# A list schedule that starts earlier in each layer of a two-layer encoder: v and g section, stores, and the order of attention and MLP steps

## The chip, the cores and the metric

The kernel runs on one core of a Trainium2 chip. The metric is device time in microseconds (us) of one execution: the median of 3 runs before the change is 1656.25 us, from 1655.57 to 1656.78 us.

## What is computed

Two layers (`DEPTH = 2`) on 512 tokens of width 1024, everything in float32. Each layer is a token part and a channel part. The reference, cut to that:

```python
for i in range(DEPTH):
    proj = x @ w_in[i]
    q_na, k_na, v_na, q_r, k_r, v_r, g_r, gate_a, gate_b = jnp.split(proj, IN_SPLITS, axis=-1)
    ya = neighbourhood_attention(q_na, k_na, v_na, na_rpb[i])          # 8 heads
    yb = bidirectional_retention(q_r, k_r, v_r, g_r, decay_f, decay_b)  # 4 heads
    merged = sigmoid(gate_a) * (ya @ w_branch_a[i]) + sigmoid(gate_b) * (yb @ w_branch_b[i])
    x = layer_norm(ALPHA * x + merged @ w_out[i], ln1_g[i], ln1_b[i])
    ffn = conv_glu_ffn(x, w_up[i], conv_w[i], conv_b[i], w_down[i])
    ple = sigmoid(x @ w_ple_gate[i]) * (p[i] @ w_ple_proj[i])
    x = layer_norm(ALPHA * x + ffn + ple, ln2_g[i], ln2_b[i])
```

## The kernel before

**Products.** Every float32 factor is split into a high and a low part: ScalarE casts the tile to `hi`, VectorE subtracts to get `lo` (`split`, L740), and each product is three matmuls (`mm3`: hi by hi, hi by lo, lo by hi). The large products are cut further, in the manner of Strassen and Winograd, into blocks of seven half-size products with the step names a, c, t1, t2, d, t3 and t4. The operands of the steps t1, t2, t3 and d are sums of halves; those of the weights are made by transfers that add in flight (GpSimd's queue, POOL), the others by VectorE. Steps of a block share PSUM banks: t4, for example, goes on adding in the bank that t3 left, so it starts only when VectorE has read that bank.

**Weights** come in chunks of 128x1024 values (512 KB) over two DMA queues: SyncE's (SP, plain loads) and POOL's (the transfers that add). They land in `raw`, `rawa` or `rawt` tiles, then come the cast `hi` on ScalarE and the subtraction `lo` on VectorE, then the matmuls.

**The order of a layer.** First the v and g section: `vg` (L1369) runs the keys of `VG[l]` (L51, L52). A key such as `0t3` is step t3 of block 0; `ga2` is one block of the a gate; `p0` and `p1` (layer 0) are the two halves of the input embedding. Then the steps of `FILL[l]` (L46): `2a` to `8t4` are blocks 2 to 8 (gates, q and k), `R0` to `R3` one step of a retention head, `N0` to `N7` one step of an attention head. `ret_head` (L1497) has four steps for each head: scores `s` and the scaled transposed keys `kz`, the states `st` and `su`, the output `o`, and the transposed output `ybt`. After the output projection and the layer norm (`proj_ln`, L1136) comes the first MLP segment in `pg` (L2140), in the order of `PG[l]` (L58): the steps a to t4 without a number are the embedding's gate, `0a` to `1t4` two blocks of the up-projection, `g` one of four plain products of it, `S` and `T` the making of sums. Then `down` (L2109) and the later segments alternate. `sums_of` (L2007) makes the sums `ss` and splits them into `sh` and `sl`, which `down` reads; `R` are the four tiles in which the residual and all products of the channel part are added.

**Who orders what.** The program is recorded first (`Program`, L226). Where `prog.plan` is 0, each engine runs its instructions as they were written. Where it is `l + 1`, a planner orders them: `_dues` (L394) gives each instruction a due time, TensorE's own being the written order at the planner's costs, and `_order` (L484) builds a list schedule from the dues, with the buffers that are free (`CAP`, L71), how far ahead of its due a load may start (`load=16` and `load=17` in `SET`, L79) and, in layer 1, a random shake of the dues (`seed=2744, shake=0.4`). TensorE may draw a later step forward, up to `prog.win` products ahead. Before the change the planner takes over behind `vg`: `prog.plan, prog.win = l + 1, FILL_WIN` (L1847), and hands back in the last MLP segment (`prog.plan = 0`, L2234). All that touches an engine passes through the recorder, so L263 stands for nearly every instruction of the profile.

Of the kernel before, what the change touches and what calls it, by code (L numbers as in the profile page):

```python
# [17 lines left out]
T = 512  # L18
# [24 lines left out]

FILL_WIN = 10
FILL_AT = (36, 40, 56, 24, 28, 8, 20)
FILL = (tuple('2a 2c 7a 7c 2t1 7t1 7t2 2t2 7d 2d 2t3 7t3 2t4 7t4 3a 8a R0 8c R1 3c R0 3t1 8t1 R1 R0 R1 8t2 8d 8t3 R0 3t2 3d 8t4 3t3 4a R1 4c 3t4 5a R2 4t1 R2 5c R3 R3 5t1 4t2 R2 4d 5t2 R2 R3 5d R3 5t3 4t3 6a 6c 6t1 N0 N1 6t2 5t4 vn 6d N3 N1 6t3 4t4 6t4 N0 vn vn bb0 N2 vn bb2 N0 N2 N5 N1 N2 N3 N4 N6 bb3 bb1 N5 N6 N6 N4 bb4 N7 bb5 N4 N5 bb6 bb7 N3 xn N7 N7'.split()),  # L46
        tuple('2a 2c 7a 7c 2t1 7t1 7t2 2t2 7d 2d 2t3 7t3 2t4 7t4 3a 8a R0 8c R1 3c R0 3t1 8t1 R1 R0 R1 8t2 8d 8t3 R0 3t2 3d 8t4 3t3 4a R1 4c 3t4 5a R2 4t1 R2 5c R3 R3 5t1 4t2 R2 4d 5t2 R2 R3 5d R3 5t3 4t3 6a 6c 6t1 N0 N1 6t2 5t4 vn 6d N3 N1 6t3 4t4 6t4 N0 vn vn bb0 N2 vn bb2 N0 N2 N5 N1 N2 N3 N4 N6 bb3 bb1 N5 N6 N6 N4 bb4 N7 bb5 N4 N5 bb6 bb7 N3 xn N7 N7'.split()))
# [7 lines left out]

TABLES_AT = ('0t4', '1t4')

PG = (tuple('a 0a T S S c 0c S t1 g g S 1a t2 1c 0t1 0t2 1t1 1t2 0d 0t3 1d 1t3 d 0t4 1t4 g t3 t4 g'.split()),  # L58
        tuple('a 0a T S S c 0c S t1 g g S 1a t2 1c 0t1 0t2 1t1 1t2 0d 0t3 1d 1t3 d 0t4 1t4 g t3 t4 g'.split()))
# [19 lines left out]
SET = {1: dict(soon=5, hold=6, reserve=10, load=16, work=25, scale=1.0, spare=2, near=10, seed=0, shake=0.0), 2: dict(soon=5, hold=6, reserve=10, load=17, work=25, scale=1.0, spare=2, near=10, seed=2744, shake=0.4)}  # L79
ROUNDS = 12  # L80


# [3 lines left out]
def _up_order(l, s):  # L86

    return UP_ORDER[l][s - 1] if s else PG[l]

# [14 lines left out]
class Root:  # L104


    def __init__(self, pool, shape, dtype, kw, options):
        self.pool, self.shape, self.dtype, self.kw = pool, list(shape), dtype, kw
        self.buf = Buf(options, [self])
        self.tile, self.log = None, []  # L110

    def alloc(self):
        if self.tile is None:
# [180 lines left out]
class Flex(Root):  # L294


    def __init__(self, choices, shape, dtype, name):
        self.shape, self.dtype, self.choices, self.tile, self.log = list(shape), dtype, choices, None, []
        self.pool, self.kw, self.label = choices[0][0], None, name

    def choose(self, i):
# [51 lines left out]
def _jobs(ops):  # L353

    jobs, cur = [], None
    bufs = set()
    for seq, o in enumerate(ops):
        if o.eng is None:
            continue
        _costs(o)  # L360
        key = (o.plan, o.win, id(o.outs[0].root)) if o.eng == "tensor" else None
        after = set()
        for x, w in [(x, False) for x in o.ins] + [(x, True) for x in o.outs]:
            for y, w2, j in x.root.log:
                if (w or w2) and x.meets(y):
                    after.add(j)
        mine = {x.root.buf for x in o.ins}
        if key is not None and cur is not None and cur[0] == key and not any(a.seq > cur[1].seq for a in after) and (o.group and o.group == cur[2] or mine <= cur[1].bufs):
            j = cur[1]
            j.members.append(o)  # L370
            j.dur += o.dur
            j.after |= after - {j}
        else:
            j = o
            j.seq = seq
            j.after = after
            j.members = [o] if key is not None else None
            j.bufs = set()
            jobs.append(j)
            if o.eng == "tensor":  # L380
                cur = (key, j, o.group)
        for x, w in [(x, False) for x in o.ins] + [(x, True) for x in o.outs]:
            x.root.log.append((x, w, j))
            j.bufs.add(x.root.buf)
    seen = set()
    for j in jobs:
        j.takes = [b for b in j.bufs if b not in seen]
        seen |= j.bufs
        for b in j.bufs:
            b.left += 1  # L390
    return jobs


def _dues(jobs):  # L394

    soon = lambda j: SET[j.plan]["soon"] if j.plan else 5
# [290 lines left out]
def trunk(tc, wpack, x_nat, x_tr, head, p_tr, rpb, decay, ln_par, ln_col, conv, cos_t, sin_t, dist, xi_d, zd, mask, ident_d, out):  # L687
    prog = Program(tc)
# [4 lines left out]
    with ExitStack() as es:  # L693
# [109 lines left out]
        def fill_items(l):  # L803
# [389 lines left out]
        for i in range(2):  # L1193
            c = slice(i * 512, (i + 1) * 512)
# [118 lines left out]
        for l in range(DEPTH):  # L1313
# [55 lines left out]
            def vg(steps):  # L1369
# [22 lines left out]

                ws.deep = VG_DEEP
                for key in VG[l]:
                    for g in steps.get(key, ()):
                        r = next(g, None)
                        if isinstance(r, dict):
                            Sx.update(r)
# [13 lines left out]
                    elif kind == "c":  # L1412
                        w = two("w")
# [158 lines left out]
            qn, kn, kl, vn = {}, {}, {}, {}  # L1572
# [126 lines left out]
            xn = []  # L1699
# [266 lines left out]
            N1, N2 = slice(0, 512), slice(512, 1024)  # L1966
# [271 lines left out]
            for s in (len(SEGS) - 1,):  # L2238
# [142 lines left out]
                w, x4 = wx["w"], wx["x"]  # L2381
# [47 lines left out]
                t4 = products("t4", x4, s == 0)  # L2429
# [158 lines left out]
```

## Time and profile before

| | before |
|---|---|
| time, median of 3 runs | 1656.25 us |
| the profiled execution's own time | 1656.36 us |
| span of its instructions, first to last | 1654.6 us |
| TensorE (PE) matmuls | 1639.7 us busy, 9765 matmuls |
| VectorE (DVE) | 1309.3 us busy |
| ScalarE (ACT) | 999.1 us busy |
| GpSimd (POOL) | 280.4 us busy |
| transfers | 352.84 MB, mean 213 GB/s |

Stages of layer 0 by the trace: v and g section up to about 122 us, `FILL` up to about 370 us, output projection to 450 us, first MLP segment to 555 us, the rest to 850 us; layer 1 repeats that, and its v and g section ends at about 943 us.

How to read it: a row of a timeline gives start, length, engine, line, operation, output<-inputs, shapes and a count; in brackets stands the idle time of the engine ahead of it and who ended that. "Busy" of PE counts a matmul from its start to its modelled end, and the next one starts before that end, so PE can be late by some tenths of a us and still look busy.

### The profile page before, as it was taken

The numbers are of one execution on the slowest core, as the hardware profiler recorded it, in microseconds if no ns is written. First come the engines' busy times: TensorE is split into PE (matmuls) and PEld (weight loads), VectorE is DVE, ScalarE is ACT, GpSimd is POOL, SyncE is SP. The second block draws the span as 40 slices with busy tenths as digits, with TensorE's granted clock in tenths as the row PEclk, the third lists the DMA queues.
The fourth block names the chain that finished last, engine by engine and source line by source line (L and its number), as shares of the span: only waits on it lengthen the run. The fifth ranks groups of instructions, "written<-read, shape, count | busy, mean of one in ns | idle before, by whom it ended". The sixth has DMA issues, their size and how long they took to land.

```text
span 1654.6 us, 25522 instructions
## 1 busy us (share of the span) xinstructions
PE 1639.7 (99%) x9765; PEld 1460.0 (88%) x9765; DVE 1309.3 (79%) x1963; ACT 999.1 (60%) x1492; POOL 280.4 (17%) x328
## 2 busy tenths in 40 slices
PE   9999999999999999999999999999999999999997
PEld 7889999888889798898888899998888897988986
DVE  7757999687878968867876489997799789687688
ACT  6756667853557556455476566688445575663554
POOL 1111222210211111111112112221002111121113
PEclk9999999999999999999999999999999999999999
DMA  8997768865698898888688857787767987989884
GB/s 307 248 263 172 168 150 211 206 185 188 167 304 230 203 277 210 229 253 204 183 225 224 228 148 177 179 203 183 214 211 186 292 235 207 269 187 276 229 173 128
DMA packets 104827, 352.84 MB, mean 213 GB/s; under 512 B 11904, under 2 KB 16512, under 8 KB 104704
## 3 DMA queue, kind: packets, MB, share of 16 engines
q0 software_dynamic: 41040, 147.34, 46.1%
q1 hardware_dynamic: 63664, 203.86, 33.6%
q8 instruction: 77, 1.26, 0.3%
q14 instruction: 46, 0.38, 0.1%
HBM read 323.89 MB, written 25.69 MB: 211 GB/s over the span
## 4 chain that ended last, share of the span: by engine, by line
PE 91%; DVE 5%; DMA 2%; issue 1%; ACT 1%; POOL 0%; DVEq 0%; POOLq 0%; ACTq 0%
PE u L263 29%; PE gt L263 22%; PE v L263 15%; PE gn L263 8%; PE w L263 8%; PE o L263 2%; PE x L263 1%; DMA rawt<-in_wpack 1%; DVE lo L263 1%; PE ns L263 1%; PE na L263 1%; PE pt L263 1%; PE s L263 1%; PE tr L263 1%; PE st L263 1%
## 5 line engine op out<-in xcount | busy, mean ns | idle before, releaser
L263 DVE TENSOR_TENSOR lo<-rawa,hi 128x1024 fp32r<-128x1024 f32 (+1 forms) x198 | 235.9, 1199 | 69.7 <-ACT hi L263 69.6
L263 POOL DMA_DIRECT2D rawa<-in_wpack x150 | 133.7, 911 | 905.6 <-DVE lo L263 689.9
L263 ACT CAST hi<-rawa 128x1024 fp32r<-128x1024 f32 (+1 forms) x198 | 202.4, 1031 | 110.3 <-DMA rawa<-in_wpack 76.6
L263 DVE TENSOR_TENSOR lo<-raw,hi 128x1024 fp32r<-128x1024 f32 (+1 forms) x159 | 191.3, 1207 | 55.3 <-ACT hi L263 55.1
L263 PE MATMUL gt<-x1t,hi 128*128 128x512 f32 x640 | 197.5, 390 | 0.0
L263 ACT CAST hi<-raw 128x1024 fp32r<-128x1024 f32 (+1 forms) x159 | 163.9, 1038 | 48.7 <-PE gn L263 17.4
L263 PEld LDWEIGHTS gt<-x1t,hi 128*128 128x128 f32 x640 | 118.9, 188 | 23.7
L263 PE MATMUL gt<-x1t,lo 128*128 128x512 f32 x320 | 124.5, 389 | 0.0
L263 PE MATMUL u<-xt,hi 128*128 128x256 f32 x448 | 81.8, 284 | 0.0
L263 PE MATMUL u<-sh,hi 128*128 128x256 f32 x288 | 81.7, 284 | 0.0
L263 PE MATMUL v<-sh,hi 128*128 128x256 f32 x288 | 81.7, 284 | 0.0
L263 PE MATMUL v<-sh,lo 128*128 128x256 f32 x288 | 81.5, 283 | 0.0
L263 PE MATMUL v<-sl,hi 128*128 128x256 f32 x288 | 81.5, 283 | 0.0
L263 PE MATMUL u<-sl,hi 128*128 128x256 f32 x288 | 81.5, 283 | 0.0
L263 PE MATMUL u<-sh,lo 128*128 128x256 f32 x288 | 81.5, 283 | 0.0
L263 PE MATMUL gn<-hi,mt 128*128 128x512 f32 x256 | 80.2, 391 | 0.0
L263 ACT ACTIVATE uh<-u 128x512 f32<-128x512 f32 x60 | 35.8, 596 | 73.2 <-PE u L263 72.9
L263 PE MATMUL gt<-ybt,hi 128*128 128x512 f32 x256 | 79.6, 392 | 0.0
L263 ACT ACT_TABLE_LOAD x46 | 59.0, 1283 | 24.6 <-DVE sl L263 9.6
L263 PE MATMUL v<-hi,sl 128*128 128x512 f32 x184 | 72.0, 391 | 1.1 <-DVE sl L263 1.1
L263 PE MATMUL v<-hi,sh 128*128 128x512 f32 x184 | 71.8, 390 | 0.3 <-ACT sh L263 0.3
L263 PE MATMUL v<-lo,sh 128*128 128x512 f32 x184 | 71.7, 390 | 0.0
(302 smaller groups left out, 4873.6 us busy)
## 6 DMA issues: line engine op xcount, KB each, us to landing
raw<-in_wpack SPq DMA_DIRECT2D x155, 512.0 KB, 6.2
rawa<-in_wpack POOLq DMA_DIRECT2D x144, 512.0 KB, 7.1
rawa<-in_wpack SPq DMA_DIRECT2D x48, 512.0 KB, 6.8
rawt<-in_wpack SPq DMA_DIRECT2D x48, 512.0 KB, 5.4
rawt<-in_wpack POOLq DMA_DIRECT2D x48, 512.0 KB, 8.9
hi<-in_wpack POOLq DMA_DIRECT2D x40, 512.0 KB, 6.4
lo<-in_wpack POOLq DMA_DIRECT2D x40, 512.0 KB, 6.2
sx<-s_scr SPq DMA_DIRECT2D x32, 512.0 KB, 8.8
```

The lines of the kernel that those rows point to most:

```text
L263: r = o.call(*[real(x) for x in o.a], **{k: real(v) for k, v in o.k.items()})
```

## The change

The planner takes over earlier: in layer 0 at the key `ga2` of the v and g section, in layer 1 at its first key `0a`. Up to the end of `vg`, TensorE keeps the written order there (`prog.win = 1`); VectorE, ScalarE and the two DMA queues are ordered by due time. In `_dues`, nothing is due later than the last product of its plan, and a store to DRAM is due 5 us behind the instruction that makes its data, where it was due by its reader before. `FILL` and `PG` have new orders in both layers, and the shake of layer 1 and its `load=17` go. The other hunks only assert, while recording, that what is read was written. The instructions of the arithmetic and the transfers stay the same, in number and size; ScalarE has 49 table loads (`ACT_TABLE_LOAD`) where it had 46.

```diff
@@ FILL (the entry of layer 1) @@
-        tuple('2a 2c 7a 7c 2t1 7t1 7t2 2t2 7d 2d 2t3 7t3 2t4 7t4 3a 8a R0 8c R1 3c R0 3t1 8t1 R1 R0 R1 8t2 8d 8t3 R0 ...
+        tuple('7a 2a 2c 7c 2t1 7t1 7t2 7d 2t2 2d 2t3 7t3 2t4 7t4 3a 8a R0 R0 3c 8c 3t1 R1 8t1 R1 R0 R1 8t2 R0 8d 8t3 ...
@@ PG (the entry of layer 1) @@
-        tuple('a 0a T S S c 0c S t1 g g S 1a t2 1c 0t1 0t2 1t1 1t2 0d 0t3 1d 1t3 d 0t4 1t4 g t3 t4 g'.split()))
+        tuple('a 0a T S c S 0c 1a g g S 1c t1 0t1 S 0t2 t2 0d 0t3 1t1 0t4 1t2 1d 1t3 d 1t4 g t3 g t4'.split()))
@@ new @@
+VG_PLAN = ("ga2", "0a")
@@ SET @@
-... 2: dict(soon=5, hold=6, reserve=10, load=17, work=25, scale=1.0, spare=2, near=10, seed=2744, shake=0.4)}
+... 2: dict(soon=5, hold=6, reserve=10, load=16, work=25, scale=1.0, spare=2, near=10, seed=0, shake=0.0)}
@@ _dues @@
-    _dues.end = now
+    ends = {j.plan: j.due for j in jobs if j.eng == "tensor"}
+    for j in jobs:
+        if j.plan:
+            j.due = min(j.due, ends[j.plan])
+            if j.dma and j.after and not any(x.parts is not None for x in j.outs):
+                j.due = min(j.due, max(a.due + a.dur for a in j.after) + soon(j))
@@ vg @@
                 for key in VG[l]:
+                    if key == VG_PLAN[l]:
+                        _Ordered.on = set()
+                        prog.plan, prog.win = l + 1, 1
@@ trunk, behind vg @@
-            _Ordered.on = set()
-            prog.plan, prog.win = l + 1, FILL_WIN
+            prog.win = FILL_WIN
```

**Place 1: VectorE at the end of the v and g section of layer 0.** The rows `p` are the additions that free the banks `u` behind step `1t3` for step `1t4`; `lo` are subtractions for later weights. Before:

```order
L263 TENSOR_TENSOR lo_944<-rawa_209,hi_943 128x1024
L263 TENSOR_TENSOR u_158_921<-u_158_921,v_765 128x512
L263 TENSOR_TENSOR u_159_922<-u_159_922,v_766 128x512
L263 TENSOR_TENSOR lo_967<-rawa_211,hi_966 128x1024
L263 TENSOR_TENSOR lo_985<-rawa_929,hi_984 128x1024
L263 TENSOR_TENSOR p_141_804<-p_141_804,u_341 128x512
L263 TENSOR_TENSOR p_141_804<-p_141_804,u_342 128x512
```

The same place now:

```order
L264 TENSOR_TENSOR u_148_921<-u_148_921,v_768 128x512
L264 TENSOR_TENSOR lo_968<-rawt_162_693,hi_955 128x1024
L264 TENSOR_TENSOR u_149_932<-u_149_932,v_778 128x512
L264 TENSOR_TENSOR lo_998<-rawa_209,hi_986 128x1024
L264 TENSOR_TENSOR p_132_806<-p_132_806,u_341 128x512
L264 TENSOR_TENSOR p_132_806<-p_132_806,u_342 128x512
L264 TENSOR_TENSOR lo_1016<-rawa_211,hi_1007 128x1024
L264 TENSOR_TENSOR lo_1032<-rawa_786,hi_1030 128x1024
```

Between the additions `u` and the additions `p` stood two subtractions `lo`; behind the last `u` there is one now, and the others follow `p`.

**Place 2: VectorE at the start of the first `down` of layer 1.** Three pairs of sums are split there; `sl` is the low half of a pair, `ss` the sums of the third pair, `R<-R,u` the first results of `down` and `R<-R,psg` gated embeddings. Before:

```order
L263 TENSOR_TENSOR lo_14121<-rawa_13727,hi_14109 128x512
L263 TENSOR_TENSOR sl_14127<-ss_14034,sh_14116 128x1024
L263 SCALAR_TENSOR_TENSOR ss_14107<-ss_14107,gg_13355 128x256
L263 TENSOR_TENSOR ss_14107<-gg_13355 128x256
L263 SCALAR_TENSOR_TENSOR ss_14107<-ss_14107,gg_13355 128x256
L263 TENSOR_TENSOR R_13112<-R_13112,u_14047 128x512
L263 TENSOR_TENSOR R_13116<-R_13116,u_14060 128x512
L263 TENSOR_TENSOR sl_14153<-ss_14107,sh_14145 128x1024
```

The same place now:

```order
L264 TENSOR_TENSOR sl_14104<-ss_14039,sh_14069 128x1024
L264 SCALAR_TENSOR_TENSOR ss_14095<-ss_14095,gg_13343 128x256
L264 TENSOR_TENSOR ss_14095<-gg_13343 128x256
L264 SCALAR_TENSOR_TENSOR ss_14095<-ss_14095,gg_13343 128x256
L264 TENSOR_TENSOR sl_14124<-ss_14043,sh_14106 128x1024
L264 TENSOR_TENSOR R_13109<-R_13109,u_14048 128x512
L264 TENSOR_TENSOR sl_14141<-ss_14095,sh_14129 128x1024
L264 TENSOR_TENSOR R_13127<-R_13127,u_14062 128x512
L264 TENSOR_TENSOR lo_14158<-rawa_13659,hi_14121 128x1024
L264 TENSOR_TENSOR R_13895<-R_13895,psg_14037 128x512
L264 TENSOR_TENSOR R_13891<-R_13891,psg_14057 128x512
```

The sums `ss` of the third pair now precede the second `sl`, and one addition to `R` moved behind the third; two multiplications of `R` by `psg` come after all three. On TensorE, `PG` now ends in `g t4` where it ended in `t4 g`: 24 matmuls of step t4 stand between the last plain product, from which the third pair is made, and `down`.

**Place 3: ScalarE in the retention heads of layer 1.** The rows `kz` scale the keys of head 1, from which TensorE makes the states `st`; `qx` is an operand of head 0's output `o`, and `wx` are decays. Before:

```order
L263 ACTIVATE kz_9957<-kz_9866,zeta 128x128 x4
L263 ACT_TABLE_LOAD
L263 ACTIVATE p_1520_9781<-p_1520_9781 128x512
L263 CAST a_9998<-ta_9845 128x512
L263 CAST a_10001<-ta_9854 128x512
L263 COPY p_1555_10007<-v_9931 128x512
L263 CAST su_10009<-st_9912 128x512
L263 CAST qx_10018<-t_1497_9674 128x512
```

The same place now:

```order
L264 ACTIVATE kz_9976<-kz_9926,zeta 128x128 x4
L264 ACT_TABLE_LOAD
L264 ACTIVATE wx_9978<-xi_sb,lgs 128x256
L264 CAST qx_10011<-t_1497_9658 128x512
L264 ACTIVATE wx_9978<-wx_9978 128x384
L264 ACTIVATE wx_9978<-xi_sb,lgs 128x256
L264 CAST hi_10030<-raw_9964 128x1024
L264 CAST a_10044<-ta_10025 128x512
L264 CAST qx_10055<-t_1510_9739 128x512
L264 CAST su_10073<-st_9998 128x512
```

The decays of head 1 moved behind its `kz`. On TensorE, 84 matmuls stood between the transposes of these keys and the states `st`; now 36 do, 24 of step `8t1` and 12 of the scores.

More of the change, by code (lines that the diff above doesn't have):

```diff
@@ L45 @@
 FILL_AT = (36, 40, 56, 24, 28, 8, 20)
-FILL = (tuple('2a 2c 7a 7c 2t1 7t1 7t2 2t2 7d 2d 2t3 7t3 2t4 7t4 3a 8a R0 8c R1 3c R0 3t1 8t1 R1 R0 R1 8t2 8d 8t3 R0 3t2 3d 8t4 3t3 4a R1 4c 3t4 5a R2 4t1 R2 5c R3 R3 5t1 4t2 R2 4d 5t2 R2 R3 5d R3 5t3 4t3 6a 6c 6t1 N0 N1 6t2 5t4 vn 6d N3 N1 6t3 4t4 6t4 N0 vn vn bb0 N2 vn bb2 N0 N2 N5 N1 N2 N3 N4 N6 bb3 bb1 N5 N6 N6 N4 bb4 N7 bb5 N4 N5 bb6 bb7 N3 xn N7 N7'.split()),
-        tuple('2a 2c 7a 7c 2t1 7t1 7t2 2t2 7d 2d 2t3 7t3 2t4 7t4 3a 8a R0 8c R1 3c R0 3t1 8t1 R1 R0 R1 8t2 8d 8t3 R0 3t2 3d 8t4 3t3 4a R1 4c 3t4 5a R2 4t1 R2 5c R3 R3 5t1 4t2 R2 4d 5t2 R2 R3 5d R3 5t3 4t3 6a 6c 6t1 N0 N1 6t2 5t4 vn 6d N3 N1 6t3 4t4 6t4 N0 vn vn bb0 N2 vn bb2 N0 N2 N5 N1 N2 N3 N4 N6 bb3 bb1 N5 N6 N6 N4 bb4 N7 bb5 N4 N5 bb6 bb7 N3 xn N7 N7'.split()))
+FILL = (tuple('2a 7a 2c 7c 7t1 2t1 2t2 7t2 2d 7d 2t3 7t3 7t4 2t4 3a 8a R0 8c R1 3c R0 3t1 8t1 R1 R0 R1 8t2 R0 8d 8t3 3t2 3d 8t4 3t3 4a R1 4c 3t4 5a R2 4t1 5c R2 R3 R3 5t1 4t2 R2 5t2 R3 R2 4d 5d 5t3 4t3 R3 6a 6c 6t1 N0 N1 6t2 5t4 vn 6d N3 N1 6t3 4t4 6t4 vn N0 bb0 N2 vn vn bb2 N0 N2 N5 N1 N3 N4 N6 bb3 N2 bb1 N4 N5 N6 N6 bb4 N7 bb5 N4 N5 xn N3 bb7 N7 bb6 N7'.split()),
+        tuple('7a 2a 2c 7c 2t1 7t1 7t2 7d 2t2 2d 2t3 7t3 2t4 7t4 3a 8a R0 R0 3c 8c 3t1 R1 8t1 R1 R0 R1 8t2 R0 8d 8t3 3t2 3d 8t4 3t3 4a R1 4c 3t4 5a R2 4t1 5c R2 R3 R3 5t1 4t2 R2 5t2 R3 R2 5d 5t3 4d 4t3 R3 6a 6c 6t1 N0 N1 6t2 5t4 vn 6d N3 N1 6t3 4t4 N0 vn 6t4 vn N2 N3 vn bb0 bb2 N0 N2 N5 N1 N2 N4 N6 N6 bb3 N4 bb1 N5 N6 bb4 N4 N7 bb5 bb7 N7 bb6 N7 N3 xn N5'.split()))
 ORD = ('vector', 'scalar', 'tensor', 'gpsimd', 'sync')
@@ L56 @@
 TABLES_AT = ('0t4', '1t4')
-PG = (tuple('a 0a T S S c 0c S t1 g g S 1a t2 1c 0t1 0t2 1t1 1t2 0d 0t3 1d 1t3 d 0t4 1t4 g t3 t4 g'.split()),
-        tuple('a 0a T S S c 0c S t1 g g S 1a t2 1c 0t1 0t2 1t1 1t2 0d 0t3 1d 1t3 d 0t4 1t4 g t3 t4 g'.split()))
+PG = (tuple('a 0a T c S g S S S g 0c 1a t1 t2 0t1 1c 0t2 0d 0t3 1t1 0t4 d g 1t2 1d 1t3 t3 1t4 g t4'.split()),
+        tuple('a 0a T S c S 0c 1a g g S 1c t1 0t1 S 0t2 t2 0d 0t3 1t1 0t4 1t2 1d 1t3 d 1t4 g t3 g t4'.split()))
 PG_EARLY = "a"
@@ L78 @@
 _SET = dict(soon=5, hold=6, reserve=10, load=16, work=25, scale=1.0, spare=2, near=10, seed=0, shake=0.0)
-SET = {1: dict(soon=5, hold=6, reserve=10, load=16, work=25, scale=1.0, spare=2, near=10, seed=0, shake=0.0), 2: dict(soon=5, hold=6, reserve=10, load=17, work=25, scale=1.0, spare=2, near=10, seed=2744, shake=0.4)}
+SET = {1: dict(soon=5, hold=6, reserve=10, load=16, work=25, scale=1.0, spare=2, near=10, seed=0, shake=0.0), 2: dict(soon=5, hold=6, reserve=10, load=16, work=25, scale=1.0, spare=2, near=10, seed=0, shake=0.0)}
 ROUNDS = 12
@@ L109, in __init__ @@
         self.buf = Buf(options, [self])
-        self.tile, self.log = None, []
+        self.tile, self.log, self.cover = None, [], 0
     def alloc(self):
@@ L297, in __init__ @@
     def __init__(self, choices, shape, dtype, name):
-        self.shape, self.dtype, self.choices, self.tile, self.log = list(shape), dtype, choices, None, []
+        self.shape, self.dtype, self.choices, self.tile, self.log, self.cover = list(shape), dtype, choices, None, [], 0
         self.pool, self.kw, self.label = choices[0][0], None, name
@@ L366, in _jobs @@
                     after.add(j)
+        for x in o.ins:
+            if x.parts is None:
+                assert any(w2 and x.meets(y) for y, w2, j in x.root.log)
+            else:
+                assert not x.mask() & ~x.root.cover
         mine = {x.root.buf for x in o.ins}
@@ L383, in _jobs @@
             x.root.log.append((x, w, j))
+            if w and x.parts is not None:
+                x.root.cover |= x.mask()
             j.bufs.add(x.root.buf)
```

## The prediction, made before the changed kernel ran

> **What bounds the kernel now.** I read the page's busy times first, then what TensorE waits for, then the timelines around those waits.
>
> ```profile
> span 1654.6 us, 25522 instructions
> PE 1639.7 (99%) x9765; PEld 1460.0 (88%) x9765; DVE 1309.3 (79%) x1963; ACT 999.1 (60%) x1492; POOL 280.4 (17%) x328
> ```
>
> TensorE is busy for 99% of the span, and the change neither adds nor removes a matmul. So it can only change the few microseconds in which TensorE has no matmul to start. The whole list of these waits in the trace:
>
> ```profile
> PE u L263 <- DVE p L263: 1.9, 2, 1.4
> PE warm L263 <- DVE warm L263: 1.2, 1, 1.2
> PE v L263 <- DVE sl L263: 1.1, 3, 0.5
> PE o L263 <- DVE qx L263: 0.7, 1, 0.7
> PE tr L263 <- DVE xn L263: 0.6, 1, 0.6
> PE v L263 <- ACT sh L263: 0.3, 1, 0.3
> PE na L263 <- DVE pt L263: 0.2, 1, 0.2
> ```
>
> Nearly every wait ends with VectorE, though VectorE is busy for 79% only: its work stands in the wrong order at a few places. No wait ends with a transfer. Without the start (warm) the list holds 4.8 us in 9 waits. That is what TensorE shows as idle; what it loses is more, as the first place tells:
>
> ```profile
> 108.33 0.39 PE L263 MATMUL u<-lo,sh 128*128 128x512 f32 x1
> 108.56 0.39 PE L263 MATMUL u<-hi,sl 128*128 128x512 f32 x1
> 110.32 0.47 PE L263 MATMUL u<-hi,xt 128*128 128x512 f32 x1 [1.37 <-DVE p L263]
> ...
> 107.21 2.36 DVE L263 TENSOR_TENSOR lo<-rawa,hi 128x1024 fp32r<-128x1024 f32 x2 [2.90 <-ACT hi L263]
> 109.49 1.28 DVE L263 TENSOR_TENSOR p<-p,u 128x512 f32<-128x512 f32 x2
> ...
> 103.79 1.28 ACT L263 ACT_TABLE_LOAD   x1 [2.11 <-DVE u L263]
> 106.14 1.98 ACT L263 CAST hi<-rawa 128x1024 fp32r<-128x1024 f32 x2
> ```
>
> Matmuls of 512 columns start 0.23 us apart (108.33, 108.56), so the next was due at 108.79 and came at 110.32: 1.53 us lost where 1.37 are shown. Each listed wait thus hides 0.16 us, and the matmul behind it often starts 0.11 us late as well (1380.91 to 1381.25 below, 0.34 for 0.23). So 4.8 + 9 x 0.16 + some 8 x 0.11 = 7.1 us can be won here, 0.43% of the time: that is the ceiling. Starts (1.2 us) and the end of the program keep their order.
>
> **The change part by part.** Durations come from the profiled execution, 1656.36 us with 1654.6 us of span; the median of the runs is 1656.25 us, 0.1 below. I sum the differences and take them from the median.
>
> *Place 1, the end of the v and g section.* VectorE frees a bank with the additions `p`, and two subtractions `lo` stand ahead of them: 2.28 us, from 107.21 to 109.49. They in turn wait for ScalarE's casts, behind a table load. The new order has one `lo` there. With one of 1.14 us fewer, `p` starts at 108.35 and the matmul at 110.32 - 1.14 = 109.18: 0.39 us lost instead of 1.53. Its cast is also one earlier in the queue, so I leave 0.2 us. In layer 1 the same pair stands ahead:
>
> ```profile
> 930.78 0.39 PE L263 MATMUL u<-hi,sl 128*128 128x512 f32 x1
> 931.70 0.47 PE L263 MATMUL u<-hi,xt 128*128 128x512 f32 x1 [0.53 <-DVE p L263]
> ```
>
> Due at 931.01, come at 931.70: 0.69 us lost, less than one `lo`, so 0 is left. Together 1.53 + 0.69 - 0.2 = **2.0 us won**; the bounds are 0 and 2.2.
>
> *A retention head of layer 0.*
>
> ```profile
> 241.25 0.40 PE L263 MATMUL o<-su,qx 128*128 128x256 f32 x2
> 242.38 0.39 PE L263 MATMUL o<-su,qx 128*128 128x256 f32 x1 [0.73 <-DVE qx L263]
> ...
> 238.10 1.22 DVE L263 TENSOR_TENSOR lo<-raw,hi 128x1024 fp32r<-128x1024 f32 x1
> 241.64 0.69 DVE L263 TENSOR_TENSOR qx<-t,qx 128x512 fp32r<-128x512 f32 x1
> ```
>
> Two matmuls 0.12 us apart end the row at 241.25, so 242.38 was due at 241.49: 0.89 us lost, and 0.1 behind it. A `lo` of 1.14 us (238.10 to 239.24) stood ahead of `qx`; in the new order the nearest `lo` follows `qx`. **1.0 us won**, bounds 0 and 1.0.
>
> *Place 2, the start of the first `down`.*
>
> ```profile
> 561.70 0.39 PE L263 MATMUL v<-lo,sh 128*128 128x512 f32 x1
> 562.41 0.50 PE L263 MATMUL v<-hi,sl 128*128 128x512 f32 x1 [0.32 <-DVE sl L263]
> ...
> 1380.27 0.39 PE L263 MATMUL v<-lo,sh 128*128 128x512 f32 x1
> 1380.91 0.50 PE L263 MATMUL v<-hi,sl 128*128 128x512 f32 x1 [0.25 <-DVE sl L263]
> 1381.25 0.40 PE L263 MATMUL v<-hi,sh 128*128 128x512 f32 x1
> ...
> 1382.40 0.39 PE L263 MATMUL v<-hi,sl 128*128 128x512 f32 x1
> 1383.05 0.50 PE L263 MATMUL v<-hi,sh 128*128 128x512 f32 x1 [0.26 <-ACT sh L263]
> 1383.39 0.40 PE L263 MATMUL v<-lo,sh 128*128 128x512 f32 x1
> 1384.31 0.50 PE L263 MATMUL v<-hi,sl 128*128 128x512 f32 x1 [0.53 <-DVE sl L263]
> ...
> 1381.77 1.29 DVE L263 TENSOR_TENSOR R<-R,u 128x512 f32<-128x512 f32 x2
> 1383.03 1.23 DVE L263 TENSOR_TENSOR sl<-ss,sh 128x1024 fp32r<-128x1024 f32 x1
> ```
>
> Layer 0 loses 0.48 + 0.11 and layer 1 loses 0.41 + 0.43 + 0.69 + 3 x 0.11: 2.5 us. Now step t4 stands between the last plain product and `down`: 24 x 0.227 = 5.4 us in which VectorE makes the third pair. And 0.6 us of `R` is moved behind the last `sl`. That covers all three waits. What is late next: the same `R` work, with two multiplications by `psg` of 0.6 us each, now falls ahead of the additions that free the banks `v` for step d. I leave 0.8 us for that, two waits of the size of 1380.91 and 1383.05: **1.7 us won**, bounds 0 (all of 2.5 us given back) and 2.5.
>
> *Place 3, retention heads of layer 1.* This is the price of the new `FILL`. The trace has the rows, not the stall:
>
> ```profile
> 994.56 1.14 ACT L263 ACTIVATE kz<-kz,zeta 128x128 fp32r<-128x128 f32 x4
> 995.72 1.28 ACT L263 ACT_TABLE_LOAD   x1
> 997.02 0.63 ACT L263 ACTIVATE p<-p 128x512 f32<-128x512 f32 x1
> ```
>
> TensorE had 84 x 0.12 = 10.1 us between the transposed keys and the states; it has 36 x 0.12 = 4.3 us now. The chain of `kz` (1.14), table load (1.30 to the next start), `wx`, the cast `qx` and VectorE's `qx` (0.6 to 0.7 each) is about 4.4 us. Started at once behind the transposes, it is in time: 0 lost. But the tile that `kz` fills is one that the 24 matmuls of `8t1` still read in the new program; then only 12 matmuls lie ahead of `st` and some 20 more ahead of `o`, 3.8 us, and `kz`, `qx` and the following `su` come late one after another, at most about 1.7 us together. Between 0 and 1.7 I take the nearest row of such a wait, `o` on `qx` at 242.38: **0.9 us lost**.
>
> *What I cost at nothing.* The waits on `xn` and `pt` (0.8 us shown) keep their place. Stores that are due at once are the same transfers on the same queue; they free tiles sooner, and no listed wait ends with a transfer. Three more table loads:
>
> ```profile
> L263 ACT ACT_TABLE_LOAD x46 | 59.0, 1283 | 24.6 <-DVE sl L263 9.6 <-DVE gg L263 7.9 <-DVE u L263 4.5
> ```
>
> 3 x 1.28 = 3.8 us of ScalarE hide in its 655 us of idle time; a load shows on TensorE only where a cast is waited for, as at place 3. There the load at 995.72 is followed by the next activation at 997.02, 1.30 us later. The Trainium skill, page "ScalarE: Activation LUTs", section "What ACT_TABLE_LOAD costs", adds a drain of about 1.38 us to each load of 1283 ns; this trace agrees on the load and shows no drain, so the sum stays with 1.30.
>
> Sum: -2.0 - 1.0 - 1.7 + 0.9 = -3.8 us. 1656.25 - 3.8 = **1652.5 us**, 0.23% below.
>
> **The rivals.** *New waits take the place of the old.* The planner moves delays, it removes no work; VectorE is as busy as before. For it speaks place 3 and the `R` work of place 2. If place 3 costs its 1.7 and place 2 gives back all it won, -2.0 - 1.0 + 1.7 = -1.3 us remain: 1655.0. Or the change does not do what it says, since the casts at place 1 follow landings and not the order: 1656.2. Against both: the casts at 106.14 waited for no landing.
>
> *Slower: loads that start too late.* In the v and g section loads now start by due time and stores stand in the same SP queue:
>
> ```profile
> 75.00:100.00 25.00, 25.00 (x112) 20.70 (x111) 12.71 (x13) 15.38 (x21) 4.35 (x5) 1.00 0.93 233
> rawa<-in_wpack POOLq DMA_DIRECT2D x144, 512.0 KB, 7.1
> ```
>
> The transfer engines are 93% busy there (the column before the last), so a load that starts late cannot catch up. One adding transfer takes 7.1 us from issue to landing; where one is issued a full landing time too late, TensorE loses up to 7.1 us, and 1652.5 becomes 1659.6. That is the point from which it decides: late loads worth over 7.1 us in sum. Against it: TensorE (25.00 of 25 us) waited for nothing there, and transfers are no busier than in stages that the planner orders already.
>
> *The drain.* With 1.38 us more behind the load of place 3, and place 3 so at 2.3 us, the sum is -2.4: 1653.9. By the page "ScalarE: Activation LUTs" of the Trainium skill it would be so; the trace speaks against it.
>
> *All waits go.* If place 3 costs nothing and all of places 1 and 2 and the head is won, -2.2 - 1.0 - 2.5 = -5.7: 1650.6.
>
> **How the numbers follow.** A measurement of this kernel can tell about 0.2%, 3.3 us, from no change: faster is below 1652.9, slower above 1659.6. The forecast (1651.6 with place 3 at 0, 1653.3 with it at 1.7, and 0.7 us each way for places 1 and 2: 1650.9 to 1654.0) has 0.56, of which 0.46 lie below 1652.9; all waits gone 0.08; new waits or no effect 0.24; the drain 0.02; slower 0.10. So faster 0.46 + 0.08 = 0.54; the same 0.10 + 0.24 + 0.02 = 0.36; slower 0.10. The range is 1650.2 to 1657.3: from the case in which all goes, to beyond the case without effect with 1 us of new waits; it leaves out the slower case and a little below.
>
> **What would show it.** In the profile after: no wait of `u` on `p` over 0.3 us at about 110 and 930 us; no wait of `v` on `sl` or `sh`; no wait of `o` on `qx` at about 241 us, but one at about 1000 us, behind a table load; short waits of `v` on `R` at about 1385 us; 49 table loads. Wrong would be a PE wait that ends with a transfer, above all before 125 us or between 850 and 950 us; waits of the old size at places 1 and 2; or PE waits that sum to more than 6 us, the present list.

## The result and the profile after

The changed kernel takes 1653.82 us (median of 20 runs, 1653.47 to 1654.62) beside 1656.03 us of the kernel before (20 runs, 1655.34 to 1657.52). The ratio is 0.9986, with a 95% interval from 0.998 to 0.9993: 2.2 us faster, which is real but less than the 0.2% that the prediction took as its bound. Forecast were 1652.5 us in a range of 1650.2 to 1657.3.

The head of the page and the whole list of TensorE's waits, of the changed kernel (columns of the list: in all, times, longest):

```profile
span 1652.4 us, 25561 instructions
PE 1639.2 (99%) x9765; PEld 1461.2 (88%) x9765; DVE 1310.2 (79%) x1963; ACT 1001.6 (61%) x1495; POOL 276.9 (17%) x328
```

```profile
PE tr L264 <- DVE xn L264: 1.3, 1, 1.3
PE warm L264 <- DVE warm L264: 1.2, 1, 1.2
PE o L264 <- DVE su L264: 1.2, 2, 0.6
PE st L264 <- DVE kz L264: 0.3, 1, 0.3
PE s L264 <- DVE qk L264: 0.2, 1, 0.2
PE o L264 <- DVE qx L264: 0.2, 1, 0.2
PE u L264 <- DVE lo L264: 0.2, 1, 0.2
```

The waits of `u` on `p`, of `v` on `sl` and `sh` and of `na` on `pt` are gone; `tr` on `xn` has doubled, and there are new ones on `su` and `kz`. Without `warm` the list sums to 3.45 us, where it had 4.78: 1.3 us fewer, and 2.2 us fewer in the span. So the list alone does not carry the comparison.

The count that does goes by the starts of the matmuls. Matmuls of 512 columns start 0.23 us apart, of 256 columns 0.12; each start that comes over 0.1 us later than that is time lost. Behind the start of the program (20 us), and by place, in us:

| kernel | v/g ends (110, 930) | attention, layer 0 | attention, layer 1 | MLP | `tr` at 1255 | rest | sum | median, us | ratio to before |
|---|---|---|---|---|---|---|---|---|---|
| before | 2.22 | 1.64 | 0.38 | 3.16 | 0.78 | 0.58 | 8.76 | 1656.03 | 1 |
| after | 0 | 1.52 | 2.45 | 1.01 | 1.51 | 0.16 | 6.65 | 1653.82 | 0.9986 [0.998, 0.9993] |
| u_start | 0.38 | 2.45 | 2.97 | 1.11 | 1.51 | 0.17 | 8.59 | 1655.83 | 0.9994 [0.9985, 1.0003] |
| u_pg | 0 | 1.65 | 2.96 | 5.90 | 1.51 | 0.17 | 12.19 | 1659.97 | 1.0019 [1.001, 1.0028] |
| u_set | 0 | 1.70 | 4.03 | 0.65 | 1.17 | 1.00 | 8.55 | 1656.48 | 1.0001 [0.9992, 1.001] |
| u_store | 0 | 3.82 | 11.38 | 0.91 | 1.51 | 0.27 | 17.89 | 1668.41 | 1.0074 [1.0061, 1.0086] |
| o_pg | 2.66 | 1.64 | 0.39 | 0.57 | 1.17 | 0.17 | 6.60 | 1652.71 | 0.9981 [0.9972, 0.999] |
| o_store | 1.38 | 1.65 | 0.39 | 4.03 | 0.83 | 0.58 | 8.86 | 1656.84 | 1.0002 [0.9993, 1.0011] |
| o_fill | 0.38 | 2.02 | 5.71 | 3.99 | 0.83 | 1.41 | 14.34 | 1662.61 | 1.0035 [1.0022, 1.0049] |
| o_seed | 1.38 | 1.65 | 1.64 | 7.12 | 1.51 | 0.17 | 13.47 | 1662.88 | 1.004 [1.0028, 1.0053] |
| r0_apart | 0 | 1.63 | 2.56 | 0.79 | 1.51 | 0.16 | 6.65 | 1654.42 | 0.9988 [0.9979, 0.9997] |
| fill00 | 0 | 1.80 | 2.84 | 0.79 | 1.51 | 0.17 | 7.11 | 1654.75 | 0.999 [0.9982, 0.9999] |
| tr_late | 0 | 1.65 | 1.22 | 1.77 | 0 | 0.97 | 5.61 | 1652.63 | 0.9977 [0.9967, 0.9986] |
| tl_o_pg | 1.38 | 1.63 | 0.38 | 0.77 | 0 | 0.17 | 4.33 | 1652.23 | 0.9977 [0.9967, 0.9986] |

Before to after this is 8.76 - 6.65 = 2.1 us, where the two profiled executions are 2.15 us apart and the medians 2.2.

The count has two limits. It leaves out the start, which differs by up to 0.8 us between these traces (the 151st matmul starts at 37.3 to 38.2 us), so sums can be compared to about half a us. And it misses matmuls of 256 columns that run while the granted clock is about half: they start 0.21 us apart, so each is only 0.09 us late. Such stretches of 3.4 us cost another 1.6 us in u_set and 1.4 us in r0_apart, both at 1001 to 1005 us, and 3.0 us in u_store, at 184 to 188 and 1044 to 1048 us. (In u_pg the matmuls of such a stretch have 512 columns, and the table counts them.) A trace shows one execution, and the runs of some kernels fall into two groups: of u_pg three took 1658.0 to 1658.2 us and eight, the traced one among them, 1659.8 to 1660.6.

The names below "after" are those of the experiments: `u_` takes one part out of the changed kernel, `o_` puts one part alone into the kernel before. Each ratio is to the runs of before beside it, whose medians were 1656.0 to 1656.5.

**What came late.** The first five rows are the layer norm on VectorE and the `tr` that waits for it, in the changed kernel; the others are place 3:

```profile
1249.14 0.68 DVE L264 SCALAR_TENSOR_TENSOR xn<-xn,gn 128x512 f32<-128x512 f32 x1
1249.74 1.22 DVE L264 TENSOR_TENSOR lo<-rawa,hi 128x1024 fp32r<-128x1024 f32 x1
1250.87 1.28 DVE L264 BATCH_NORM_STATS2 bn<-xn 128x6 f32<-128x512 f32 x2
...
1253.81 0.39 PE L264 MATMUL gn<-hi,mt 128*128 128x512 f32 x1
1255.54 1.07 PE L264 MATMUL tr<-ident,xn 128*128 128x128 f32 x8 [1.34 <-DVE xn L264]
...
995.30 0.89 ACT L264 ACTIVATE kz<-kz,zeta 128x128 fp32r<-128x128 f32 x3 [1.10 <-PE v L264]
996.61 0.37 ACT L264 ACTIVATE kz<-kz,zeta 128x128 fp32r<-128x128 f32 x1 [0.42 <-DVE kz L264]
997.00 1.28 ACT L264 ACT_TABLE_LOAD   x1
998.29 0.51 ACT L264 ACTIVATE wx<-xi_sb,lgs 128x256 f32<-128x256 f32 x1
998.71 0.60 ACT L264 CAST qx<-t 128x512 fp32r<-128x512 f32 x1
...
999.36 0.51 PE L264 MATMUL o<-su,qx 128*128 128x256 f32 x2
1000.09 0.39 PE L264 MATMUL o<-su,qx 128*128 128x256 f32 x1 [0.22 <-DVE qx L264]
...
1004.25 0.28 PE L264 MATMUL o<-su,qx 128*128 128x256 f32 x1
1005.16 0.51 PE L264 MATMUL o<-su,qx 128*128 128x256 f32 x2 [0.63 <-DVE su L264]
```

In the chain of the layer norm a `lo` of 1.13 us (1249.74 to 1250.87) now stands between the residual and its statistics. In the kernel before they followed at once, behind two `lo`:

```profile
1248.79 2.35 DVE L263 TENSOR_TENSOR lo<-rawa,hi 128x1024 fp32r<-128x1024 f32 x2
1251.06 0.68 DVE L263 SCALAR_TENSOR_TENSOR xn<-xn,gn 128x512 f32<-128x512 f32 x1
1251.65 1.28 DVE L263 BATCH_NORM_STATS2 bn<-xn 128x6 f32<-128x512 f32 x2
```

The place of this one `lo` does not explain the longer wait: between the statistics of the tile before and those of this one VectorE runs four `lo` in both kernels. The kernel before lost 0.41 us at 1248.93 us, where a product `gn` needed one of them, and 0.78 at `tr`, 1.19 together; the changed kernel loses 1.51 at `tr` alone, and o_pg, with a `lo` at the same place, 1.17. Where the 0.3 us come from stays open.

At place 3 the chain that the prediction drew is there: `kz` waits until the matmuls `v` are done (1.10 us; that they are those of `8t1`, which still read its tile, is the prediction's reading of the program), then come the load, `wx`, and `qx`. Lost are 0.36 us at `st`, 0.71 at the first `o` and 0.89 at 1005.16. The last of these waits for `su` and has its like in layer 0, at 185.42 us (0.81 lost), where the first steps of the heads stand as before; that it hangs on the load is not shown.

### The profile page after: what moved, and what is told of

The parts are those of the page before. It is cut to its first block, busy times and chain, and to the rows that moved or that the text cites. A ratio compares the mean times of both kernels' runs of the same rounds, so it can differ in the third digit from the quotient of the medians.

```text
span 1652.4 us, 25561 instructions
## 1 busy us (share of the span) xinstructions
PE 1639.2 (99%) x9765; PEld 1461.2 (88%) x9765; DVE 1310.2 (79%) x1963; ACT 1001.6 (61%) x1495; POOL 276.9 (17%) x328
## 4 chain that ended last, share of the span: by engine, by line
PE 92%; DVE 4%; ACT 1%; DMA 1%; issue 1%; POOL 0%; DVEq 0%; POOLq 0%; ACTq 0%
PE u L264 30%; PE gt L264 23%; PE v L264 16%; PE gn L264 9%; PE w L264 7%; PE o L264 1%; PE x L264 1%; DVE lo L264 1%; PE ns L264 1%; PE na L264 1%; PE pt L264 1%; DMA gb_scr<-p 1%; PE tr L264 1%; DVE t L264 1%; DVE R L264 0%
```

## The experiments

### One part taken out of the change

**u_start: the list schedule begins behind the v and g section again.**

```diff
-                    if key == VG_PLAN[l]:
-                        _Ordered.on = set()
-                        prog.plan, prog.win = l + 1, 1
...
-            prog.win = FILL_WIN
+            _Ordered.on = set()
+            prog.plan, prog.win = l + 1, FILL_WIN
```

> The changed kernel, but the list schedule of a layer begins behind the v and g section again, as before the change; all else stays changed. Theory A (each part of the change moves the waits of its own place): the waits of u on p at about 110 and 930 us come back, 2.2 us lost, and nothing else: 1653.8 + 2.2 = 1656.0. Rival B (the stores that are due at once carry the gain, since they free tiles sooner): the stores stay due at once behind the section, so the time stays at 1653.8. Rival C (any edit deals all waits of a layer anew): the u on p waits are back, but waits at other places come and go as well, and the total may be anything from 1653 to 1658.

Measured: 1655.83 us. The sum is that of theory A, the places are not. Only 0.38 us come back at 110 and 930 us, 0.19 at each. The rest is 0.9 us in the attention of layer 0 (1.70 us are lost at 133 to 134 us, where the changed kernel loses nothing; its own 0.81 at 185 us are gone) and 0.5 in that of layer 1. So the early start is worth 2 us, but hardly at its own place.

Why place 1 stays nearly clear is to be read from ScalarE. Its instructions there stand in the same order in o_store (old `FILL`) and in u_start, but for what the table load waits for. The timelines, o_store first:

```profile
102.92 1.28 ACT L264 ACT_TABLE_LOAD   x1 [2.36 <-DVE u L264]
104.21 1.15 ACT L264 ACTIVATE g<-u 128x512 f32<-128x512 f32 x2
```

```profile
100.99 1.28 ACT L264 ACT_TABLE_LOAD   x1
103.29 0.63 ACT L264 ACTIVATE g<-u 128x512 f32<-128x512 f32 x1 [1.02 <-DVE u L264]
```

In o_store the load, which needs no data, carries a wait for VectorE, and the first activation behind it waits, by its semaphores, for ScalarE's own work alone. In u_start the load has no wait and runs in the idle time, and the activation waits for VectorE itself. The casts behind it, and so `p`, come earlier, and 0.69 us lost become 0.19.

**u_pg: the old order `PG`.** The edit puts the two old tuples of `PG` back.

> The changed kernel, but with the old order PG at the start of the first down section in both layers. Theory A: waits of v on sl or sh come back at about 560 and 1380 us, and the short waits of v on R at about 1388 us go: 3.1 us lost there instead of 0.8, so 1653.8 + 2.3 = 1656.1; the places at 110 and 930 us stay clear. Rival B (stores due at once carry the gain): 1653.8. Rival C (waits are dealt anew everywhere): waits of layer 1 at 997 to 1006 and 1255 us change as well.

Measured: 1659.97 us, 6.1 us above the changed kernel. All parts but `PG` together are slower than the kernel before. Place 2 loses more than it did there. TensorE and the windows (length, busy time of PE, PEld, DVE, ACT and POOL, then granted clock, share of the transfers and GB/s) at the first `down` of layer 1:

```profile
1382.93 0.50 PE L264 MATMUL v<-hi,sh 128*128 128x512 f32 x1 [0.88 <-ACT sh L264]
...
1384.47 0.50 PE L264 MATMUL v<-hi,sl 128*128 128x512 f32 x1 [0.80 <-DVE sl L264]
...
1385.78 0.63 PE L264 MATMUL v<-hi,sh 128*128 128x512 f32 x1
1386.21 0.63 PE L264 MATMUL v<-lo,sh 128*128 128x512 f32 x1
```

```profile
1383.00:1385.00 2.00, 1.20 (x4) 0.71 (x5) 2.00 (x3) 2.00 (x3) 0.00 (x0) 1.00 0.88 127
1385.00:1388.50 3.50, 3.50 (x10) 2.66 (x9) 3.42 (x4) 1.77 (x3) 0.87 (x1) 0.53 0.02 2
```

The two waits lose 1.04 and 0.97 us, and behind them seven matmuls start 0.43 us apart, from 1385.35 to 1388.34 us, at a granted clock of 0.53. That alone is 7 x 0.2 = 1.4 us.

**u_set: the old numbers of layer 1's planner.**

```diff
-SET = {... 2: dict(... load=16, ... seed=0, shake=0.0)}
+SET = {... 2: dict(... load=17, ... seed=2744, shake=0.4)}
```

> The changed kernel, but layer 1 is planned with the old numbers again (a random shift of up to 0.4 us of each due time, loads reserved from 17 instead of 16). Theory A: these numbers belong to no place; place 1 and the start of the first down section stay as in the changed kernel in layer 0, and the waits of layer 1 change by chance: 1653.8 plus or minus 1. Rival D (taking the random shift away carries the gain): without it layer 1 is back at its old loss, 1653.8 + 2.2 = 1656.0.

Measured: 1656.48 us, 2.7 above the changed kernel: theory A's bound of 1 us is missed, and by this run alone rival D would be right. Layer 0 is nearly as it was (1.70 us lost instead of 1.52 in its attention); layer 1 loses 3.93 us at its heads instead of 1.96, and behind them 1.6 us more at about half the granted clock (0.57 from 1001.00 to 1005.00 us). The counterpart o_seed, below, decides.

**u_store: stores due by their readers again.**

```diff
-            if j.dma and j.after and not any(x.parts is not None for x in j.outs):
-                j.due = min(j.due, max(a.due + a.dur for a in j.after) + soon(j))
```

> The changed kernel, but a store has the due time that its reader gives it, as before, and not at once. As the prediction put it, stores due at once cost and win nothing: 1653.8 plus or minus 0.5, and no matmul waits for what a transfer holds up. Rival B (the stores carry the gain, or are what makes the early start possible): late stores keep tiles, so loads start later; casts of ScalarE then wait for landings, and 2 us or more come back: 1656 or above, most of it where the list schedule now begins earlier, in the v and g section of layer 1 at 850 to 950 us.

Measured: 1668.41 us, 14.6 above the changed kernel. Rival B's second half is right, that the rule for stores makes the early start possible; its place, 850 to 950 us, is not. The four stores of `pp` (the packed embeddings) in the trace, first of the changed kernel, then of u_store (length of an issue, then the first and the last start):

```profile
L264 SPq DMA_DIRECT2D r_scr<-pp x4: 404/1051/1360, 839.0 to 841.7; - x4
```

```profile
L264 SPq DMA_DIRECT2D r_scr<-pp x4: 442/480/937, 942.2 to 1023.7; - x4
```

The reader of these stores is the MLP, far behind, so due by it they go 100 to 180 us later, and the four tiles stay taken through the retention heads. Most of the losses stand there: 10.4 us between 953 and 1044 us, at 12 places, the first of them:

```profile
953.76 0.39 PE L264 MATMUL v<-sh,lo 128*128 128x256 f32 x1 [1.02 <-DVE lo L264]
```

The attention of layer 0 loses 2.3 us more than in the changed kernel. With the table's 11.2 us more in all, and the 3.0 us at half clock that it does not count, 14.2 of the 14.6 us are found. No matmul waits for a transfer here either; VectorE and ScalarE are late. That the taken tiles make them late is how I read it; the runs show the late stores and the loss together, and that nothing else was edited.

### One part alone

Except for o_seed, these kernels also have the cap of `_dues`, by which nothing is due later than the last product of its plan; o_store, which has it, takes the time of the kernel before. Neither the early start alone nor the change without the new `FILL` was run.

**o_pg: the new `PG` in the kernel before.**

> The kernel before with one part of the change alone, the new order PG at the start of the first down section. Theory A (each part moves the waits of its own place, a planned layer around it stays): the waits of v on sl and sh at about 560 and 1380 us go, 3.1 us, and at most 0.8 comes back as waits of v on R: 1656.0 - 2.3 = 1653.7, as fast as the whole change; the waits of u on p at 110 and 930 us and of o on qx at 242 us stay. Rival C (the planner deals the waits of a layer anew): waits of VectorE elsewhere come in their place, 1655 to 1657.

Measured: 1652.71 us, no slower than the whole change. Its waits:

```profile
PE u L264 <- DVE p L264: 2.3, 2, 1.8
PE warm L264 <- DVE warm L264: 1.2, 1, 1.2
PE tr L264 <- DVE xn L264: 1.0, 1, 1.0
PE o L264 <- DVE qx L264: 0.7, 1, 0.7
PE v L264 <- DVE R L264: 0.3, 1, 0.3
```

As theory A has it, the waits on `sl` and `sh` are gone (MLP 3.16 to 0.57 us), one on `R` is left, and the places at 110, 242 and 930 us stay. The attention of layer 1 keeps its 0.39 us. The trace is of an execution 1.0 us above the median: 1.97 us are lost at 110 us, since a `rawt` landed late (its cast at 100.19 us waited 1.41 us for it). `PG` alone brings what the whole change brings.

**o_store: the rule for stores alone** (the two lines of u_store's diff, with the cap, added to the kernel before).

> The kernel before with the stores due at once alone. Theory A': stores due at once are a condition for the early start and win nothing by themselves, since without that start no load waits for a tile that a store keeps: 1656.0 plus or minus 0.5, with the list of waits as before. Rival B (they carry the gain): 1653.8.

Measured: 1656.84 us, a ratio of 1.0002 with an interval across 1. Theory A' holds in time: the stores of `pp` go at 841 to 844 us with and without the rule, as long as the list schedule begins behind the section. Its list of waits does not hold: in the MLP of layer 1 two waits on `lo` are new and two on `sh` and `sl` gone, and the MLP of both layers loses 0.9 us more in this trace.

**o_fill: the new `FILL` of both layers alone.**

> The kernel before with the new order FILL of both layers alone. Theory A (place 3 is the price of layer 1's FILL, the head at 242 us the gain of layer 0's): no wait of o on qx at 242 us, 1.0 won; 2.0 lost at 985 to 1006 us: 1656.0 - 1.0 + 2.0 = 1657.0. Rival G (place 3 is the price of the early start, which leaves VectorE and ScalarE with other work when the heads begin): nothing lost at 985 to 1006 us, 1656.0 - 1.0 = 1655.0. Both keep the waits at 110, 560, 930 and 1380 us.

Measured: 1662.61 us. Both expectations are wrong in size. Theory A's places hold in the attention: no wait at 242 us, and 2.4 us lost from 983 to 1005 us, so the loss needs no early start. But 3.3 us more are lost from 1028 to 1057 us, and 1.27 at 134 us, near where u_start loses 1.70 and the changed kernel nothing. The places at 110 and 930 us lose 0.19 each, not 0.69: it is the new `FILL` under which the table load no longer waits.

**o_seed: the new numbers of layer 1's planner alone.**

> The kernel before with the new numbers of layer 1's planner alone: no random shift of due times, loads reserved from 16. Rival D (the shift cost time, and taking it away carries the gain): 1656.0 - 2.2 = 1653.8. Theory A (the numbers belong to an order, and the old ones to the old order): the old order of layer 1 loses by it, as the new order lost 2.7 us by the old numbers: 1657 to 1660, all of it behind 850 us.

Measured: 1662.88 us, slower by more than theory A gave. Rival D falls. With u_set:

| | old numbers | new numbers |
|---|---|---|
| old order and start | 1656.0 | 1662.9 |
| new order and start | 1656.5 | 1653.8 |

Neither set is the better one. Each was good for the order that it stood with.

### Place 3, and the wait of `tr`

**r0_apart: the first two steps of head 0 apart again, in layer 1.**

```diff
-3a 8a R0 R0 3c 8c 3t1 R1 8t1 R1 R0 R1 8t2 R0 8d
+3a 8a R0 8c R1 3c R0 3t1 8t1 R1 R0 R1 8t2 R0 8d
```

> The changed kernel, but in layer 1 of FILL the first two steps of retention head 0 stand apart again, as before the change (3a 8a R0 8c R1 3c R0 3t1 8t1 instead of 3a 8a R0 R0 3c 8c 3t1 R1 8t1). The prediction's mechanism for place 3: with 84 matmuls instead of 36 between the transposed keys and the states, the waits at 997 to 1006 us (1.96 us lost) go: 1653.8 - 2.0 = 1651.8. Rival F (the wait is not one of distance, since VectorE and ScalarE take the planner's order and a table load stands in it wherever the step is): some 1 to 2 us stay lost at about 1000 us, and the time stays within 0.7 of 1653.8.

Measured: 1654.42 us; the traced execution took 1655.48. Rival F holds. `st` no longer waits, but 2.56 us are lost at the next products, and behind them the granted clock is about half for 3.4 us, which costs 1.4 us more (the last row is a window, in the columns given at u_pg):

```profile
999.56 0.35 PE L264 MATMUL o<-vh,a 128*128 128x256 f32 x1 [1.54 <-DVE ta L264]
...
995.01 1.28 ACT L264 ACT_TABLE_LOAD   x1
996.31 0.53 ACT L264 ACTIVATE wx<-wx 128x384 f32<-128x384 f32 x1
996.74 1.12 ACT L264 CAST a<-ta 128x512 fp32r<-128x512 f32 x2
...
1001.30:1004.70 3.40, 3.40 (x16) 3.40 (x17) 3.21 (x5) 2.23 (x4) 0.00 (x0) 0.51 0.54 113
```

The distance between the keys and the states was restored, and the wait moved to the first `o`. By the trace that waits for a `ta` of VectorE, which stands there behind the two `a`, and these stand behind a table load.

**fill00: layer 0's entry of `FILL` for layer 1 too.**

> The changed kernel, but layer 1 runs through its attention steps in layer 0's new order of FILL (7t1 ahead of 2t1, head 0's first two steps apart, bb6 last). Theory A (the loss at 997 to 1006 us hangs on layer 1's own FILL): layer 0 has none at the same steps, so the 1.96 us go: 1653.8 - 2.0 = 1651.8. Rival G (it hangs on the early start and the tiles that are free then): 1 to 2 us stay lost at 985 to 1010 us, 1653.8 plus or minus 0.7.

Measured: 1654.75 us; 1.71 us are lost at 986 to 1005 us and 1.13 at 1027 to 1043. Theory A falls: the steps of heads 0 and 1 stand here as in the kernel before, but for head 0's last one, which is now ahead of `8d`, and the loss stays.

**tr_late: the changed kernel with layer 1's first transposes 24 matmuls later.**

```diff
-                if t:
-                    done(t - 1)
+                if t and not (late and t == 1):
+                    if late and t == 2:
+                        done(0)
+                    done(t - 1)
```

> The changed kernel, but in layer 1 the eight transposes tr of the first token tile are issued behind the next token tile's 24 matmuls, 5.4 us later. Theory A: the wait of tr on xn at 1255.54 us, 1.51 us lost, is covered, and the rest stays: 1653.8 - 1.5 = 1652.3. Rival C: the planner orders layer 1 anew round this edit, and other waits of layer 1 (997 to 1006 us, 1385 us) change too: 1650.5 to 1656. Rival E (the chain behind tr is as tight): the first products of the MLP wait for the splits of the tile instead, and 1653.8 stays.

Measured: 1652.63 us. The 1.51 us are gone, and rival E falls. But layer 1 is ordered anew, as rival C has it: its attention loses 1.2 us less, the MLP and the rest 1.6 more, 0.8 of them at a `gn` just ahead of `tr` (1246.21 us). That the time is near theory A's 1652.3 is partly chance.

**tl_o_pg: `PG` alone with the same late transposes.**

> The kernel before with the new order PG alone and, as a second edit, the first token tile's transposes tr of layer 1 issued 24 matmuls later. PG alone took 1652.7 us and has 1.17 us lost where tr waits for xn at 1255.40 us. Theory A: that goes, and the waits at 110, 242, 930 and 1388 us stay: 1652.7 - 1.2 = 1651.5. Rival C (layer 1 is ordered anew round the edit): 1651 to 1654, with waits of layer 1 that PG alone doesn't have; layer 0 is as with PG alone in both cases.

Measured: 1652.23 us. The 1.17 us of o_pg go, and only 0.2 us in the MLP come in their place:

```profile
PE warm L264 <- DVE warm L264: 1.2, 1, 1.2
PE u L264 <- DVE p L264: 1.1, 2, 0.5
PE o L264 <- DVE qx L264: 0.7, 1, 0.7
PE na L264 <- DVE pt L264: 0.2, 1, 0.2
```

With 4.33 us lost in the trace this is the least of all kernels here, and with tr_late the fastest. Its ratio of 0.9977 [0.9967, 0.9986] beside the changed kernel's 0.9986 [0.998, 0.9993] leaves open by how much it beats that one; the medians are 1.6 us apart. Theory A's 1651.5 is missed: each beside its own runs of before, the medians are 4.1 us (tl_o_pg) and 3.8 us (o_pg) lower, so they show 0.3 of the 1.17 us. Why not more stays open.

## Why the prediction was right, and where it was wrong

The time was within the range and 1.3 us above the forecast; the sum was 3.8 us won where 2.2 were. The prediction gave 0.54 to a time below 1652.9 us, and 0.36 to what came, a change of less than 0.2%. Term by term, from the traces of before and after:

- *Place 1, 2.0 won.* 2.22 in the trace: the size is right, but in part by luck. Of the 2.22 us, 0.84 belong to the profiled execution of before, in which a `rawt` landed late: three other traces of the same instructions (o_store, o_seed, tl_o_pg) lose 0.69 us at 110 us, not 1.53, and a fourth (o_pg), with a later landing still, 1.97. The prediction went by the casts at 106.14 us, which waited for no landing; a cast ahead of them did. The cast of that tile, in the kernel before and in o_store:

```profile
99.67 1.05 ACT L263 CAST hi<-rawt 128x1024 fp32r<-128x1024 f32 x1 [0.98 <-DMA rawt<-in_wpack]
```

```profile
98.56 1.05 ACT L264 CAST hi<-rawt 128x1024 fp32r<-128x1024 f32 x1
```

  Another 1.00, 0.50 at each place, goes with the new `FILL` alone (o_fill), under which the table load no longer waits, and the early start takes the last 0.38. That split holds only for this order of adding the parts. In layer 1 of the changed kernel the prediction's own reason is at work: the load waits for VectorE again, but no `lo` stands just ahead of `p`, and VectorE idles until TensorE has filled the bank. The kernel before, then the changed one:

```profile
925.17 1.28 ACT L263 ACT_TABLE_LOAD   x1 [2.37 <-DVE u L263]
928.60 2.36 DVE L263 TENSOR_TENSOR lo<-rawa,hi 128x1024 fp32r<-128x1024 f32 x2 [2.14 <-ACT hi L263]
930.87 1.28 DVE L263 TENSOR_TENSOR p<-p,u 128x512 f32<-128x512 f32 x2
...
922.62 1.28 ACT L264 ACT_TABLE_LOAD   x1 [1.30 <-DVE u L264]
927.29 0.69 DVE L264 TENSOR_TENSOR p<-p,u 128x512 f32<-128x512 f32 x1 [2.25 <-PE u L264]
```

- *The head of layer 0, 1.0 won.* 0.99, as forecast. Not priced were new waits in the heads of that layer: 0.81 us at 185 us, 0.22 at 217, and 0.25 more at 166.
- *Place 2, 1.7 won.* 3.16 to 1.01 in the MLP: 2.15, the size a little low because late starts that the list of waits does not show were not counted (0.48 us at 557.65 us, the largest). The mechanism is shown by o_pg, which does it alone, and the 0.79 us left in layer 1 are the 0.8 that were forecast, though 0.44 of them wait for a `lo` and not behind `R`.
- *Place 3, 0.9 lost.* **This step was mis-sized:** 2.45 us are lost in the attention of layer 1, 1.96 of them at the place itself, above the bound of 1.7. The reason given, 36 matmuls instead of 84 between keys and states, covers at most the 0.36 us at `st`: with the distance restored (r0_apart, fill00) `st` no longer waits, but 2.56 and 2.84 us are lost in that attention all the same. Every trace with the new `FILL` loses over 1 us there, with or without the early start; with the old `FILL` and the old numbers, nothing (before, o_pg, o_store, tl_o_pg). Which of its steps does it, head 0's last step ahead of `8d` in both layers among them, was not tried and stays open.
- *At nothing: "the waits on `xn` and `pt` keep their place".* **This step failed.** At `tr` on `xn` 0.73 us more are lost, while the 0.41 us lost at `gn` just ahead of it went, and `na` on `pt` no longer costs its 0.8 us. Together 0.5 us are won, which is luck.
- *At nothing: the stores.* Right for the stores by themselves (o_store), wrong as a statement on the change: without their rule the changed kernel takes 14.6 us more (u_store).

The sum of what was measured: -2.22 - 0.99 - 2.15 + 2.45 + 0.73 - 0.8 - 0.4 + 1.3 = -2.1 us. Place 3 (1.5 us more than forecast) and layer 0's heads (1.3) make the miss; place 2 and the waits on `pt` and `lo` gave part of it back. So the forecast's mechanisms and the rival in which new waits take the place of the old were both at work.

Of the signs that the prediction named, all were seen: no wait of `u` on `p` or of `v` on `sl` and `sh`, none of `o` on `qx` at 241 us but one at 1000.09 behind a load, a late start of 0.24 us at 1388.75 (too short for the list; o_pg's list puts the same place down to `R`), no wait ended by a transfer, and a list below 6 us. They did not guard against the waits at 185 and 1005 us, which no sign covered.

Of the rivals: the slower one did not happen, no matmul waits for a transfer. The drain did not either, although its 1653.9 us is nearest to what came; that is luck: the load at 997.00 us is followed by the next activation at 998.29, 1.29 us later. The Trainium skill, page "ScalarE: Activation LUTs", section "What ACT_TABLE_LOAD costs", adds about 1.38 us there; this trace shows none of it.

## What to carry to other kernels

Where one engine is 99% busy and a planner orders the others, the effects of the parts do not add: `PG` brought over 3 us to the old kernel and 6 to the rest of the change, and the random numbers were right only for the order that they stood with. So test each part of such a change alone and keep what wins by itself; here one order of one section won all of it. A total that comes out as expected (u_start) does not show that the places did.

## What the hardware showed beside that

- A table load on ScalarE can carry a wait for data that it does not need; then it starts only when they are there, and its 1.28 us come on top. The same load without the wait ran in the idle time ahead (at 100.99 us, where it was 102.92). Whether that costs TensorE anything depends on what follows: at 922.62 us in the changed kernel the load waited, and nothing was lost.
- Two waits of TensorE close together can cost more than their length: in u_pg, 2.0 us lost within 3.4 us were followed by a stretch of 3.5 us at a mean granted clock of 0.53, with 0.43 us from start to start. The Trainium skill, page "TensorE: Matmul & The Clock Gate", section "Wait — 56ns, not 53.3ns?", gives 426.7 ns for 512 columns at half clock, and the trace agrees. By the section "What's actually happening" of the same page of the Trainium skill the clock falls after an idle window of about 3.4 us; here TensorE had started five matmuls in the 3.4 us ahead, so a partly idle stretch was enough. The length of the waits does not settle it: in o_seed 3.4 us are lost at 1343.70 and 1345.65 us, and the granted clock stays at 1.00 behind them.
- A late landing moved the loss at one place from 0.69 to 1.53 and to 1.97 us between executions of the same instructions. A wait behind a transfer, read from one execution, carries such an error.
